# Two-layer decoder trunk on one core: the first mixer's tile slots counted by use, pole scalars in pairs, phase doublings for both layers at once, more gelu copies on ScalarE

## The chip, the core and the metric

The kernel runs on one core of a Trainium2 chip. The time is the device's own, from start to end of one execution, in microseconds (us). Five engines work side by side, each through its own instructions in the order in which they are written, and wait for one another through semaphores: TensorE (PE) multiplies matrices and transposes, VectorE (DVE) and ScalarE (ACT) do elementwise work, GpSimd (POOL) does little here, and SyncE (SP) issues the DMAs. PE's clock is granted by the chip, at full speed (shown as 1.00) or at half of it.

## The reference, cut to what matters

The trunk has two layers of three sub-layers each: a SwiGLU feed-forward block, a mixer, and another feed-forward block, each between two RMS norms and scaled, shifted and gated by rows made from a conditioning vector. There are 256 positions of width 1024, in float32.

```python
for l in range(DEPTH):                       # 2
    x = post_add(x, swiglu(pre(x, 0), ...), 0, FFN_RES)
    y = token_mixer(pre(x, 1), ...)
    x = post_add(x, y, 1, 1.0)
    x = post_add(x, swiglu(pre(x, 2), ...), 2, FFN_RES)

def token_mixer(h, ...):
    u, q, k, v, f, g_a, g_b = split(h @ w_in)
    y_ssm = s5_ssm(u, ...)                   # complex diagonal recurrence over the positions
    z_val, z_gate = split(gelu(y_ssm) @ glu_w)
    y_a = z_val * sigmoid(z_gate)
    y_b = forgetting_attention(q, k, v, f + forget_b) @ attn_w_out
    return (sigmoid(g_a) * y_a + sigmoid(g_b) * y_b) @ w_out
```

`s5_ssm` has 32 groups of 64 complex poles, `lam_bar = exp(lam * dt)`; each state is the last one times `lam_bar` plus an input, and the output is read from the states. The attention has 8 heads of width 64 (4 pairs), with a forget term added to the logits, and a causal mask.

## The kernel before

**Weights.** All weights come as 512 tiles of 128x1024 in one fixed order, `raw0`, `raw1`, ..., each by one DMA. 368 hold weights, 144 ("mod") go into the conditioning rows. To keep float32 precision a weight tile is split: ACT rounds it (`Stream.hi`, line 359, `hi<-raw`), DVE takes the rest (`Stream.lo`, line 372, `lo<-raw,hi`), and PE forms each product in three matmuls, hi·xh, lo·xh and hi·xl. A mod tile costs one DVE instruction (`raw<-raw,crow`, summed into `mc`). SBUF has 42 slots for such tiles (`SLOTS`), shared by the stream and all other big tiles. How far the stream may run ahead is set by `room` (line 351):

```python
return SLOTS - self.kept - (TABLES[self.kb.stage] if self.kb.stage is not None else 0)
```

`kept` is what the stage reserves for itself (`KEPT`), `TABLES` what the building of the recurrence's tables takes in its two stages. At the u projection, before the tables are loaded, `mix_body` (line 946) reserves `KEPT["mix1"] - LATER`.

**The order.** A planner in the kernel (`Plan`, line 164) steps through the program with costs of its own, and writes every engine's instructions in the order in which its clocks would take them. The chip then runs each engine's list strictly in that order, so an instruction that waits holds all behind it. Nearly all instructions are recorded with one line, that of the planner's call, so the names of the tiles tell them apart.

**The mixer.** After the projections v, f, q, k and u come, for each of the four head pairs: scores on PE (`sc<-kt,qt`), the logits' six DVE operations (`lg<-nbd..`), two reduces (`st<-lg`), the exponentials on ACT, a reciprocal on DVE, the normalising on ACT, PE transposes (`sc<-kc,lg`), a copy on ACT (`lg<-sc`), the values on PE (`sc<-lg,v`), and their split into `ath` on ACT and `atl` on DVE. In between PE runs the gate projections ga1, gb0 and gb1 as filler (48 matmuls each; their tiles are 138 to 143, 144 to 149 and 151 to 156). The recurrence takes tables: `bt` turns the spread inputs `U` into `vr` and `vi` (32 matmuls in 16 + 16), `w` is a table of phases that `scan` (line 1257) applies with 12 products of 128x1024 before and after two scans on DVE (first operation `zr<-w,vr`, last one `zr<-zr,t`), `d` adds the part of a chunk's own inputs (`ys<-U,d`), and `c` reads the outputs (`ys<-zr,c`, two groups of 32 matmuls, after the scan). `gelu` (line 1283) takes each half of ys through ACT and copies it to a new layout in 16 small copies of 32x128 (`yg<-g`), then splits it into `ygh` (ACT) and `ygl` (DVE). `yb` is the attention's output projection (tiles 158, 159, 161, 163), `z` the gelu's (tiles 164 to 173), `mt` transposes the merged result, and `ym` is the mixer's output projection. The gating row `gT` is transposed on PE when the mod tiles up to 167 are summed in `mc`.

**Where the tables come from.** `s5_scalars` (line 1384) computes poles, powers and factors for both layers with DVE operations of 128x32, in the first feed-forward block. `s5_tables` (line 1712) builds a layer's tables: layer 0's from the end of that block into mixer 0, layer 1's in the third feed-forward block. Its last step is `s5_w` (line 1540), the phases `wc` and `ws` by six doublings; for five of them the next factor is computed by 11 operations of 128x16 (tile `pw`). The tables are written to HBM and loaded back (`load_tables`, line 1152, and `w<-sw`).

Of the kernel before, what the change touches and what calls it, by code (L numbers as in the profile page):

```python
# [9 lines left out]
F32 = mybir.dt.float32  # L10
F32R = mybir.dt.float32r
I32 = mybir.dt.int32
AF = mybir.ActivationFunctionType
# [25 lines left out]
TABLES = (11, 8)  # L39
# [7 lines left out]
LATER = 4  # L47
# [366 lines left out]
class Kern:  # L414
# [868 lines left out]
    def gelu(self, h, ys, out):  # L1283
# [100 lines left out]
    def s5_scalars(self):  # L1384
# [17 lines left out]
        x1, x2, x3, x4, ur, ui, lre2 = (new() for _ in range(7))  # L1402
# [17 lines left out]
        cth, sth = new(), new()  # L1420
        q, mm_, z = new(), new(), new()
# [41 lines left out]
        def cmul(ore, oim, a, b, t1=t1, t2=t2, t3=t3, t4=t4):  # L1463
            tt(t1, a[0], b[0], M)
            tt(t2, a[1], b[1], M)
            tt(t3, a[0], b[1], M)
            tt(t4, a[1], b[0], M)
            tt(ore, t1, t2, S)
            tt(oim, t3, t4, A)

        LP, NP_, LI = self.spw[:, 0], self.spw[:, 1], self.spw[:, 2]

        def neg(o, a):
            ts(o, a, -1.0, M)

        def powers(i):
            return LP[:, i, :], LI[:, i, :]

        def part3():
            tt(LP[:, 0, :], e, cth, M)  # L1480
            tt(LI[:, 0, :], e, sth, M)
            cmul(*powers(1), powers(0), powers(0))
            cmul(*powers(2), powers(1), powers(0))
            cmul(*powers(3), powers(1), powers(1))
            for i in range(4):
                neg(NP_[:, i, :], LP[:, i, :])
                neg(self.spw[:, 3, i, :], LI[:, i, :])
# [16 lines left out]
        def part5():  # L1504
# [14 lines left out]
            neg(self.sq[:, 2, :], self.sq[:, 1, :])  # L1519
# [20 lines left out]
    def s5_w(self, l):  # L1540
# [5 lines left out]
        p = self.r4("pw")[:, 0:256].rearrange("p (n j) -> p n j", j=16)  # L1546
# [3 lines left out]
        pr, pi = self.sw4[:, 0, 16 * l:16 * l + 16], self.sw4[:, 1, 16 * l:16 * l + 16]  # L1550
        done = v.take()
        for i in range(6):
            n = 1 << i
# [11 lines left out]
            large = v.take()  # L1565
            if i < 5:
                a, b, x, y = (p[:, 4 * (i % 2) + d, :] for d in range(4))
                tt(x, pr, pr, M)
                tt(y, pi, pi, M)
                tt(b, pr, pi, M)  # L1570
                tt(a, x, y, S)
                tt(b, b, b, A)
                tt(x, a, a, M)
                tt(y, b, b, M)
                tt(x, x, y, A)
                v.tensor_scalar(x, x, -0.5, 1.5, op0=M, op1=A)
                tt(a, a, x, M)
                tt(b, b, x, M)
                pr, pi = a, b
            small = v.take()  # L1580
            v.mix(large, small)
            done += v.take()
        v.ops = done
# [80 lines left out]
    def s5_c(self, l):  # L1664
        v3 = lambda c: self.bc[:, 512 + 256 * c:768 + 256 * c].rearrange("p (j n) -> p j n", j=16)
        self.cp = [self.r4(n).rearrange("p (j s n) -> p j s n", j=16, s=4) for n in ("cpr", "cpi")]
        yield from self.powers(self.cp, 0, 4, (v3(0), v3(1)), [self.spw[:, n, :, 16 * l:16 * l + 16] for n in (0, 3, 3, 1)],
# [44 lines left out]
    def s5_tables(self, l):  # L1712
# [25 lines left out]
        if self.s == 1:  # L1738
            self.load_tables()
# [221 lines left out]
```

## Time and profile before

| | us |
|---|---|
| three runs | 1184.0, 1187.42 (median), 1192.24 |
| the profiled execution | 1182.35 |
| span of its records | 1180.6 |
| PE busy | 1140.6 (97%) |
| DVE busy | 912.7 (77%) |
| ACT busy | 608.6 (52%) |
| mean granted clock of PE | 0.992 |

The shares are means over stages that differ: the feed-forward blocks keep PE busy all the time, the mixers don't. A timeline row gives start, duration and instruction, and in brackets how long its engine was idle just before and what ended that. Neighbouring instructions of one engine overlap a little, so the step from one start to the next is shorter than a duration. Times in the rows count from the start of the span.

### The profile page before, as it was taken

How to read it: one execution, taken by the hardware profiler on the slowest of the kernel's cores; microseconds unless marked ns; L12 is line 12 of the kernel's file. 1: busy time of each engine (PE TensorE's matmuls, PEld its weight loads, DVE VectorE, ACT ScalarE, POOL GpSimd, SP SyncE). 2: the span in 40 equal slices, each digit the busy share in tenths (PEclk: the TensorE clock that was granted, in tenths of full speed). 3: DMA queues.
4: the chain of work that ended last, by engine and by line, in shares of the span. 5: the costliest groups of instructions: out<-in, count | busy, mean ns of one | idle time of the engine just before them, and what ended most of it. 6: DMA issues, size and time to landing. Idle time of an engine off the chain costs nothing.

```text
span 1180.6 us, 19407 instructions
## 1 busy us (share of the span) xinstructions
PE 1140.6 (97%) x7488; PEld 1015.5 (86%) x7488; DVE 912.7 (77%) x1529; ACT 608.6 (52%) x943; POOL 36.2 (3%) x62
## 2 busy tenths in 40 slices
PE   8999999998998999999999999999999999999997
PEld 5999998796786779999979989987987887999995
DVE  6988987897998889999678878878448798855532
ACT  5653452685556564444364475356355756543421
POOL 1000000000000010000010000001000001000000
PEclk9999999998999999999999999999999999999999
DMA  9999887577887669999769398966645566765300
GB/s 361 408 367 407 301 286 267 187 257 236 339 306 249 224 235 390 360 376 381 246 214 355 127 330 284 373 248 237 227 127 179 180 212 216 284 224 204 126 19 36
DMA packets 99186, 306.50 MB, mean 260 GB/s; under 512 B 16373, under 2 KB 26133, under 8 KB 99094
## 3 DMA queue, kind: packets, MB, share of 16 engines
q1 hardware_dynamic: 99094, 305.27, 71.6%
q8 instruction: 58, 0.95, 0.3%
q14 instruction: 34, 0.28, 0.1%
HBM read 291.51 MB, written 13.71 MB: 259 GB/s over the span
## 4 chain that ended last, share of the span: by engine, by line
PE 86%; DVE 7%; ACT 3%; DMA 2%; issue 2%; POOL 1%; SPq 0%; DVEq 0%; POOLq 0%; ACTq 0%
PE f L128 35%; PE y L128 20%; PE n L128 5%; PE ym L128 3%; PE ga L128 3%; PE gb L128 3%; PE z L128 3%; PE k L128 2%; PE q L128 2%; PE v L128 2%; PE ys L128 2%; PE u L128 2%; ACT xh L128 1%; DVE raw L128 1%; PE yb L128 1%
## 5 line engine op out<-in xcount | busy, mean ns | idle before, releaser
L128 DVE TENSOR_TENSOR lo<-raw,hi 128x1024 fp32r<-128x1024 f32 x368 | 437.1, 1218 | 27.2 <-ACT hi L128 21.3
L128 ACT ACTIVATE hi<-raw 128x1024 fp32r<-128x1024 f32 x367 | 370.7, 1055 | 68.3 <-PE f L128 38.7
L128 PE MATMUL f<-xl,hi 128*128 128x256 f32 x1216 | 341.4, 281 | 2.7 <-DVE xl L128 2.7
L128 PE MATMUL f<-xh,hi 128*128 128x256 f32 x1216 | 342.0, 281 | 1.9 <-ACT xh L128 1.9
L128 PE MATMUL f<-xh,lo 128*128 128x256 f32 x1216 | 341.0, 280 | 0.0
L128 PEld LDWEIGHTS f<-xh,lo 128*128 128x128 f32 x1216 | 232.4, 191 | 0.0
L128 PEld LDWEIGHTS f<-xl,hi 128*128 128x128 f32 x1216 | 228.4, 188 | 4.6 <-DVE xl L128 3.6
L128 PEld LDWEIGHTS f<-xh,hi 128*128 128x128 f32 x1216 | 228.5, 188 | 3.8 <-ACT xh L128 2.5
L128 PE MATMUL y<-hi,ht 128*128 128x512 f32 x704 | 196.2, 391 | 0.8 <-DVE yg L128 0.8
L128 DVE SCALAR_TENSOR_TENSOR raw<-raw,crow 128x1024 f32<-128x1024 f32 x144 | 173.3, 1218 | 6.0 <-DMA raw<-ws 5.9
L128 PEld LDWEIGHTS y<-hi,ht 128*128 128x128 f32 x704 | 129.3, 188 | 26.2 <-DVE yg L128 1.1
L128 ACT ACTIVATE sg<-f 128x512 f32<-128x512 f32 x38 | 22.7, 597 | 222.7 <-PE f L128 215.4
L128 PE MATMUL y<-lo,ht 128*128 128x512 f32 x352 | 109.3, 390 | 0.8 <-ACT yg L128 0.8
L128 DVE TENSOR_TENSOR sg<-sg,f 128x512 f32<-128x512 f32 x38 | 26.1, 687 | 90.0 <-ACT sg L128 89.9
L128 PEld LDWEIGHTS y<-lo,ht 128*128 128x128 f32 x352 | 66.1, 188 | 15.1 <-ACT yg L128 1.2
L128 PE MATMUL n<-hi,xl 128*128 128x512 f32 x96 | 37.9, 395 | 1.7 <-DVE xl L128 1.7
L128 ACT ACTIVATE lg<-lg,st 128x128 f32<-128x128 f32 (+1 forms) x64 | 26.1, 444 | 25.3 <-DVE st L128 25.3
L128 PE MATMUL n<-hi,xh 128*128 128x512 f32 x96 | 38.4, 400 | 0.0
L128 PE MATMUL n<-lo,xh 128*128 128x512 f32 x96 | 37.7, 392 | 0.0
L128 DVE TENSOR_TENSOR yg<-y,row 128x1024 f32<-128x1024 f32 (+1 forms) x9 | 9.9, 1103 | 32.8 <-ACT xn L128 23.6
L128 DVE TENSOR_TENSOR ht<-sg,ht 128x512 fp32r<-128x512 f32 x38 | 26.1, 687 | 9.8 <-ACT ht L128 9.5
L128 ACT ACTIVATE xh<-xt,mc 128x128 fp32r<-128x128 f32 x80 | 21.7, 383 | 22.1 <-PE xt L128 22.1
(276 smaller groups left out, 1646.7 us busy)
## 6 DMA issues: line engine op xcount, KB each, us to landing
raw<-ws SPq DMA_DIRECT2D x512, 512.0 KB, 5.8
row<-sg SPq DMA_DIRECT2D x11, 512.0 KB, 8.0
sbt<-bT SPq DMA_DIRECT2D x8, 512.0 KB, 3.0
sc<-cd SPq DMA_DIRECT2D x16, 256.0 KB, 8.0
bt<-sbt SPq DMA_DIRECT2D x8, 512.0 KB, 4.5
c<-sc SPq DMA_DIRECT2D x8, 512.0 KB, 10.2
d<-sd SPq DMA_DIRECT2D x4, 512.0 KB, 4.6
w<-sw SPq DMA_DIRECT2D x4, 512.0 KB, 5.8
```

Of the source, the lines that this page charges most:

```text
L128: r = f(*a, **k)
```

## The change

It has three parts.

1. **Slots.** `TABLES` goes from (11, 8) to (9, 0) and `LATER` from 4 to 15. While the layer 0 phases are built, at the u projection, the stream's room is 42 − 8 − 9 = 25 where it was 42 − 19 − 11 = 12 (by the code's own numbers). Before the tables are loaded in a mixer, a loop waits until the slots in use fit.
2. **Scalars.** Real and imaginary parts stand side by side, so that one operation of 128x64 does both (`product`, `square`). Negations and the copies to `srv` go to ACT. All six phase factors are computed for both layers at once in `part4`, 7 rounds of 8 operations, and `s5_w` loses its 110 small operations (55 per layer).
3. **Gelu copies.** 12 of 16 per half run on ACT, 4 on DVE, where it was 8 and 8.

In all DVE has 117 instructions fewer (1386 to 1269, expanded), ACT 22 more (889 to 911), PE, POOL and SP as many as before.

```diff
-TABLES = (11, 8)
+TABLES = (9, 0)
...
+OVER = 0
+LATER = 15
...
-                if t % 2:
+                if t:
                     yield "act", g
                     nc.scalar.activation(o, i, AF.Copy)
...
-        def cmul(ore, oim, a, b, t1=t1, t2=t2, t3=t3, t4=t4):
...
+        def product(out, a, b):
+
+            tt(tp, a, b, M)
+            tt(t3, a[:, 0], b[:, 1], M)
+            tt(t4, a[:, 1], b[:, 0], M)
+            tt(out[:, 0], t1, t2, S)
+            tt(out[:, 1], t3, t4, A)
+
+        def square(out, a, xp=None):
+            x = tp if xp is None else xp
+            tt(x, a, a, M)
+            tt(out[:, 1], a[:, 0], a[:, 1], M)
+            tt(out[:, 0], x[:, 0], x[:, 1], S)
+            tt(out[:, 1], out[:, 1], out[:, 1], A)
...
         def part4():
-            unit = (cth, sth)
-            for out in ((ur, ui), (self.sw4[:, 0, :], self.sw4[:, 1, :])):
-                cmul(lre2, th, unit, unit, x1, x2, x3, x4)
-                tt(x1, lre2, lre2, M)
-                tt(x2, th, th, M)
+            unit = up
+            for i in range(7):
+                out = wp if i == 0 else self.sw4[:, i - 1]
+                square(zp, unit, xp)
+                tt(xp, zp, zp, M)
                 tt(x1, x1, x2, A)
                 ts(x1, x1, -0.5, M, 1.5, A)
-                tt(out[0], lre2, x1, M)
-                tt(out[1], th, x1, M)
+                tt(out, zp, x1[:, None, :].to_broadcast([P, 2, W]), M)
                 unit = out
...
-            for n, src in enumerate((LP, LI, self.spw[:, 3])):
-                for i in range(3):
-                    v.tensor_copy(self.srv[:, n, i, :], src[:, 2 - i, :])
+            for i in range(3):
+                act(self.srv[:, :, i, :], self.spw[:, 1:4, 2 - i, :], AF.Copy)
...
-            if i < 5:
-                a, b, x, y = (p[:, 4 * (i % 2) + d, :] for d in range(4))
...
         if self.s == 1:
+            self.st.kept = KEPT["mix1"]
+            while self.st.used() > SLOTS - self.st.kept + OVER:
+                yield "dve", self.plan.clk["pe"] + 0.5
             self.load_tables()
```

Because the planner writes the order, the first part moves instructions on all engines in mixer 0. On DVE, where the scan starts, before had these rows (`lo` with its `raw` tile's number; `st` are the softmax's sums):

```order
L128 TENSOR_REDUCE st_508_3594<-lg_507_3593 128x2 x2
L128 TENSOR_SCALAR st_508_3594<-st_508_3594 128x4
L128 TENSOR_TENSOR lo_509_3604<-raw146_435_3011,hi_495_3540 128x1024
L128 TENSOR_TENSOR lo_510_3610<-raw148_454_3186,hi_500_3550 128x1024
L128 RECIPROCAL st_508_3594<-st_508_3594 128x4
L128 TENSOR_TENSOR lo_511_3613<-raw149_455_3188,hi_503_3580 128x1024
L128 TENSOR_TENSOR zr_492_3536<-w_489_3529,vr_487_3447 128x1024
L128 TENSOR_TENSOR t_494_3538<-w_490_3531,vi_488_3448 128x1024
```

In the changed order the low parts of tiles 149 to 163, the mod rows 152 to 167 and the softmax of head pair 2 come first. From the middle of that stretch:

```order
L129 TENSOR_TENSOR lo_522_3602<-raw158_472_3249,hi_520_3594 128x1024
L129 SCALAR_TENSOR_TENSOR raw157_470_3242,mc_82<-raw157_470_3242,crow_73 128x1024
L129 SCALAR_TENSOR_TENSOR raw160_490_3400,mc_82<-raw160_490_3400,crow_73 128x1024
L129 SCALAR_TENSOR_TENSOR raw162_501_3505,mc_82<-raw162_501_3505,crow_73 128x1024
L129 TENSOR_TENSOR lo_534_3674<-raw159_489_3398,hi_532_3670 128x1024
L129 TENSOR_TENSOR atl_493_3442<-sc_496_3461,ath_492_3441 128x256
L129 TENSOR_TENSOR lo_538_3701<-raw161_495_3452,hi_536_3697 128x1024
L129 SCALAR_TENSOR_TENSOR raw165_511_3565,mc_82<-raw165_511_3565,crow_73 128x1024
```

After it come the six logits' operations of pair 2, and then the end of the stretch:

```order
L129 TENSOR_REDUCE st_541_3710<-lg_540_3709 128x2 x2
L129 TENSOR_SCALAR st_541_3710<-st_541_3710 128x4
L129 SCALAR_TENSOR_TENSOR raw167_516_3581,mc_82<-raw167_516_3581,crow_73 128x1024
L129 TENSOR_TENSOR mc_82<-mc_82,kc_74 128x8
L129 SCALAR_TENSOR_TENSOR mc_82<-mc_82,kc_74 128x8
L129 RECIPROCAL st_541_3710<-st_541_3710 128x4
L129 TENSOR_TENSOR lo_546_3752<-raw163_505_3532,hi_544_3748 128x1024
L129 TENSOR_TENSOR zr_529_3647<-w_526_3640,vr_518_3591 128x1024
```

The scan's first product moved behind the low parts of 151 to 163 and the sums of head pair 2; the mod row 167 and its `mc`, which stood behind the gelu, moved ahead of it.

On ACT, these rows of the changed order feed that stretch (`lg<-sc` is the copy of a head pair's transposes, here pair 1's; `ath` the split of its values):

```order
L129 ACTIVATE hi_515_3579<-raw156_469_3238 128x1024
L129 ACTIVATE hi_520_3594<-raw158_472_3249 128x1024
L129 ACTIVATE lg_497_3468<-sc_496_3461 128x2x384
L129 ACTIVATE hi_532_3670<-raw159_489_3398 128x1024
L129 ACTIVATE ath_492_3441<-sc_496_3461 128x256
L129 ACTIVATE hi_536_3697<-raw161_495_3452 128x1024
```

In before, hi of 159 came after the copy of pair 3's transposes, and its lo after the scan.

On PE, between the last gate matmuls and the first matmuls that need the scan (`ys<-zr,c`), before had:

```order
L128 MATMUL gb1_530_3736<-hi_524_3693,xl_72 128x512
L128 MATMUL ys_544_3838<-U_468_3281,d_461_3231 128x64 x8
L128 MATMUL ys_544_3838<-U_468_3281,d_462_3232 128x64 x8
L128 MATMUL yb_547_3861<-hi_532_3757,ath_481_3414 128x512 x2
L128 MATMUL yb_547_3861<-lo_540_3817,ath_481_3414 128x512 x2
L128 MATMUL yb_547_3861<-hi_532_3757,atl_482_3415 128x512 x2
L128 MATMUL ys_544_3838<-zr_492_3536,c_512_3624 128x63
```

and the changed order has:

```order
L129 MATMUL gb1_513_3569<-hi_515_3579,xl_72 128x512
L129 MATMUL ys_551_3767<-U_474_3291,d_483_3367 128x64 x8
L129 MATMUL ys_551_3767<-U_474_3291,d_484_3368 128x64 x8
L129 MATMUL sc_535_3695<-kc_74,lg_540_3709 128x128 x6
L129 MATMUL sc_552_3791<-kt_442_3061,qt_411_2861 128x128 x2
L129 MATMUL sc_552_3791<-kt_442_3061,qt_411_2861 128x256 x2
L129 MATMUL sc_535_3695<-lg_540_3709,v_343_2423 64x128 x6
L129 MATMUL sc_552_3791<-kc_74,lg_554_3798 128x128 x6
L129 MATMUL sc_552_3791<-lg_554_3798,v_343_2423 64x128 x6
L129 MATMUL yb_557_3848<-hi_520_3594,ath_492_3441 128x512 x2
L129 MATMUL yb_557_3848<-lo_522_3602,ath_492_3441 128x512 x2
L129 MATMUL yb_557_3848<-hi_520_3594,atl_493_3442 128x512 x2
```

Nine more yb rows follow, and then `ys<-zr,c`. The last two head pairs and twelve yb rows, where it was three, now stand ahead of the scan's first reader. Two further moves on PE are not shown: the 32 matmuls of vr and vi, which stood ahead of the last quarter of ga1, now stand behind all of ga1 and gb0 and the first quarter of gb1; and gT stands in the middle of z where it stood behind it.

## Rows read from the trace of the kernel before

**Rows 1.** The page's part 1: busy us (share of the span), instructions.
```profile
PE 1140.6 (97%) x7488; PEld 1015.5 (86%) x7488; DVE 912.7 (77%) x1529; ACT 608.6 (52%) x943; POOL 36.2 (3%) x62
```

**Rows 2.** Windows: from:to us, length, busy us (instructions) by engine, clock, DMA, GB/s.
```profile
46.00:206.00 160.00, 160.00 (x1122) 149.46 (x1121) 138.13 (x276) 74.88 (x95) 1.77 (x5) 1.00 0.90 332
236.00:394.00 158.00, 141.87 (x952) 121.58 (x951) 141.54 (x300) 99.45 (x185) 1.16 (x2) 0.97 0.78 276
620.00:797.00 177.00, 176.38 (x1271) 162.52 (x1271) 146.53 (x260) 94.21 (x138) 2.36 (x4) 1.00 0.78 286
```

**Rows 3.** PE's waits: who waited for whom, total us, times, longest.
```profile
PE z L128 <- ACT ygh L128: 4.8, 1, 4.8
...
PE gT L128 <- DVE mc L128: 2.8, 1, 2.8
...
PE ga L128 <- DVE lo L128: 2.3, 1, 2.3
...
PE ga L128 <- ACT hi L128: 1.4, 1, 1.4
...
PE z L128 <- DVE ygl L128: 0.5, 1, 0.5
```

**Rows 4.** PE's timeline, mixer 0: start us, us, instruction, [idle before].
```profile
276.89 0.50 PE L128 MATMUL ga<-hi,xh 128*128 128x512 f32 x1
...
295.49 0.43 PE L128 MATMUL vr<-U,bt 128*128 128x64 f32 x2
...
302.68 0.82 PE L128 MATMUL sc<-kc,lg 128*128 128x128 f32 x6
...
344.04 0.43 PE L128 MATMUL ys<-zr,c 128*128 128x63 f32 x2 [0.64 <-DVE zr L128]
...
371.28 1.22 PE L128 MATMUL z<-hi,ygh 128*128 128x512 f32 x2 [4.79 <-ACT ygh L128]
...
393.03 0.70 PE L128 MATMUL ym<-hi,xh 128*128 128x512 f32 x2
```

**Rows 5.** The chain of waits, mixer 0: start us, us, what.
```profile
286.88 5.06 PE ga L128 x11
...
296.25 1.55 DVE lg L128 x6
297.80 0.93 DVE st L128 x2
...
298.96 1.87 ACT lg L128 x8
...
310.93 5.80 DMA w<-sw
...
329.14 2.77 PE gb L128 x12
```

**Rows 6.** DVE's timeline in the first scan.
```profile
315.06 1.21 DVE L128 TENSOR_TENSOR zr<-w,vr 128x1024 f32<-128x1024 f32 x1
...
327.73 1.22 DVE L128 TENSOR_TENSOR zi<-zi,t 128x1024 f32<-128x1024 f32 x1
328.87 2.28 DVE L128 TENSOR_TENSOR_SCAN zr<-r,zr 128x1024 f32<-128x1024 f32 x1
...
342.77 1.22 DVE L128 TENSOR_TENSOR zr<-zr,t 128x1024 f32<-128x1024 f32 x1
```

**Rows 7.** ACT's timeline, beside it.
```profile
315.47 1.99 ACT L128 ACTIVATE hi<-raw 128x1024 fp32r<-128x1024 f32 x2
...
326.93 1.49 ACT L128 ACTIVATE lg<-lg,st 128x128 f32<-128x128 f32 x4
```

**Rows 8.** Tile pw, all operations: count, duration ns min/median/max, first and last start.
```profile
L128 DVE TENSOR_TENSOR pw<-pw x94: 143/166/178, 274.4 to 767.2; 128x16 f32<-128x16 f32 x94
```

**Rows 9.** Tile yg, the two kinds of gelu copy, same columns.
```profile
L128 ACT ACTIVATE yg<-g x32: 424/430/441, 348.5 to 940.5; 32x128 f32<-32x128 f32 x32
L128 DVE COPY yg<-g x32: 266/274/279, 351.9 to 941.3; 32x128 f32<-32x128 f32 x32
```

More of the change, by code (lines that the diff above doesn't have):

```diff
@@ L46 @@
 NEAR = 1
-LATER = 4
+OVER = 0
+LATER = 15
 SCAN, GELU, MERGE, TR = 0.5, 0.95, 0.5, 1.5
@@ L1401, in s5_scalars @@
         t1, t2, t3, t4 = new(), new(), new(), new()
-        x1, x2, x3, x4, ur, ui, lre2 = (new() for _ in range(7))
+        x1, x2, x3, x4, ur, ui, lre2, th2 = (new() for _ in range(8))
+        pair = lambda n: T[:, n:n + 2, :]
+        tp, xp, wp, zp = pair(4), pair(8), pair(12), pair(14)
         def exp(out, x):
@@ L1420, in s5_scalars @@
         cth, sth = new(), new()
+        up = pair(16)
         q, mm_, z = new(), new(), new()
@@ L1461, in part2 @@
             tt(sth, sth, z, A)
-        def cmul(ore, oim, a, b, t1=t1, t2=t2, t3=t3, t4=t4):
[L1464 to L1474, printed above, removed]
+        def product(out, a, b):
[10 more added lines that the diff above has]
+            tt(out[:, 1], out[:, 1], out[:, 1], A)
+        act = lambda *a, **k: v.ops.append((self.nc.scalar.activation, a, k))
+        NP_, LP, LI, NI = (self.spw[:, i] for i in range(4))
         def powers(i):
-            return LP[:, i, :], LI[:, i, :]
+            return self.spw[:, 1:3, i, :]
         def part3():
@@ L1481, in part3 @@
             tt(LI[:, 0, :], e, sth, M)
[L1482 to L1487, printed above, removed]
+            square(powers(1), powers(0))
+            product(powers(2), powers(1), powers(0))
+            square(powers(3), powers(1))
+            act(NP_, LP, AF.Copy, scale=-1.0)
+            act(NI, LI, AF.Copy, scale=-1.0)
             r4 = self.sr4.rearrange("p l j -> p (l j)")
@@ L1518, in part5 @@
             tt(self.sq[:, 1, :], t3, q, M)
-            neg(self.sq[:, 2, :], self.sq[:, 1, :])
+            act(self.sq[:, 2, :], self.sq[:, 1, :], AF.Copy, scale=-1.0)
         def part6():
-            for n, src in enumerate((LP, LI, self.spw[:, 3])):
-                for i in range(3):
-                    v.tensor_copy(self.srv[:, n, i, :], src[:, 2 - i, :])
+            for i in range(3):
+                act(self.srv[:, :, i, :], self.spw[:, 1:4, 2 - i, :], AF.Copy)
         def part(*fs):
@@ L1549, in s5_w @@
         tt = lambda o, a, b, op: v.tensor_tensor(o, a, b, op=op)
-        pr, pi = self.sw4[:, 0, 16 * l:16 * l + 16], self.sw4[:, 1, 16 * l:16 * l + 16]
-        done = v.take()
         for i in range(6):
+            pr, pi = (self.sw4[:, i, k, 16 * l:16 * l + 16] for k in range(2))
             n = 1 << i
@@ L1564, in s5_w @@
             tt(s1, s1, t2, A)
-            large = v.take()
-            if i < 5:
-                a, b, x, y = (p[:, 4 * (i % 2) + d, :] for d in range(4))
[L1568 to L1583, printed above, removed]
         yield from v.run()
@@ L1666, in s5_c @@
         self.cp = [self.r4(n).rearrange("p (j s n) -> p j s n", j=16, s=4) for n in ("cpr", "cpi")]
-        yield from self.powers(self.cp, 0, 4, (v3(0), v3(1)), [self.spw[:, n, :, 16 * l:16 * l + 16] for n in (0, 3, 3, 1)],
+        yield from self.powers(self.cp, 0, 4, (v3(0), v3(1)), [self.spw[:, n, :, 16 * l:16 * l + 16] for n in (1, 3, 3, 0)],
                     self.r4("ct"))
@@ L1761, in run @@
             self.sq = cst.tile([P, 3, 32], F32, name="sq")
-            self.sw4 = cst.tile([P, 2, 32], F32, name="sw4")
+            self.sw4 = cst.tile([P, 6, 2, 32], F32, name="sw4")
             self.sr4 = cst.tile([P, 2, 16], F32, name="sr4")
```

1 line of the change is left out of this document (removed).

## The prediction

> **What bounds the kernel now.** The page's first part comes first: TensorE (PE) is busy for 1140.6 of 1180.6 us, VectorE (DVE) for 912.7, ScalarE (ACT) for 608.6 [rows 1]. So nothing that shortens DVE or ACT can pay unless PE waits for them, and all that can be won is 40 us of PE idle plus what a low clock costs. Then the windows say where PE waits. In the first feed-forward stage (46 to 206) it is busy for 160.00 of 160 us, in a later one (620 to 797) for 176.38 of 177; from the first mixer's last third of projections to the end of its gates (236 to 394) for 141.87 of 158, at a granted clock of 0.97, with DVE busy for 141.54 [rows 2]. Here DVE is as full as PE, and the two wait for each other. The list of PE's waits names the places: z for the rounded gelu output ygh 4.8 us, the row transpose gT for mc 2.8, ga for lo 2.3 and for hi 1.4 [rows 3]. The chain adds one: after ga's wait eleven matmuls took 5.06 us, where twelve of the same shape take 2.77 [rows 5]; that is the 1.2 GHz level of the clock, some 2.5 us lost.
>
> All of this lies in mixer 0, and the change edits mixer 0. Outside it I read the edits as hidden.
>
> **Edits outside the mixer: 0.** The pair packing, the negations on ACT and the doublings for both layers stand in the first feed-forward stage. DVE loses 23 small operations there and gains 32; at 0.17 us, the nearest recorded size [rows 8], the nine more are +1.5 us, with bounds of −4 (the 32 as good as free) and +5 (none saved). DVE has 22 us of slack in that stage and PE has none [rows 2], so nothing moves; if the cover were gone it would be those 1.5 us. ACT gets 6 copies on 75 us of work in 160. Layer 1's table phases lose 55 operations of 128x16, 94 recorded for both layers at 166 ns [rows 8], in the stage where PE is busy for 176.38 of 177 us: hidden too.
>
> **Edits in mixer 0, walked by hand.** I took the changed order of PE, DVE and ACT, gave each instruction the start-to-start time of its like in the trace of before, and let each start when its engine and its inputs are free. PE: a 512-wide matmul 0.229, so 12 are 2.75 [rows 5]; the 32 vr/vi are 7.2 (295.49 to 302.68), a transpose set or scores about 0.9 [rows 4]. DVE: a 1024-wide operation 1.14, a scan 2.2 [rows 6]; the six lg operations 1.55 and their two reduces 1.0 [rows 5]. ACT: the exponentials of one head pair 1.87 [rows 5], hi or a copy of its size 1.0, normalising 1.4 [rows 7].
>
> *The front.* ga1 starts at 276.89 [rows 4]. All its low parts now stand ahead of the table phases on DVE, so its 48 matmuls run through to about 288.0: the 1.4 and 2.3 us waits and the slow clock, 6.2 us, are gone. Waits for the softmax of pair 0 (2.1) and the score sets bring PE to 293.2; 24 of gb0 to 298.7; a wait for lo148, behind the phases, 1.3; the rest of gb0 and 12 of gb1 to 307.9; vr/vi to 315.1. In before vr/vi were done at 302.68 [rows 4], since they stood ahead of those 36 gate matmuls.
>
> *The scan start.* This is the term that decides. DVE runs the low parts up to lo158, then lo159. Its input hi159 stands on ACT behind the copy lg<-sc of pair 1, which waits for PE's transposes of pair 1, which stand behind vr/vi. Transposes 315.9, copy 316.7, hi159 317.7, lo159 318.9; atl after values(1) 320.3; lo161 and a mod row 323.2. Scores(2) end on PE at 323.2, lg and reduces at 326.0, exponentials 327.9, the gb1 copy 328.9, normalising 330.3, hi163 331.3, lo163 332.5. Only then does DVE reach zr<-w,vr, the scan's first product; in before it starts at 315.06 [rows 6]. So the scan starts 17.4 us later. It then has less between its operations: 12 products and 2 scans are 18.1, one lg set 2.6, two atl 0.7, one low part 1.1, small waits 1.0, together 23.5, against 28.9 in before (315.06 to 342.77 and the last product's 1.22), which has five low parts in it. It ends at 356.0, 12 later than 344.0.
>
> *After the scan.* PE waits meanwhile (about 3 us for the gb1 copy, 3 for scores(3), 6.7 for pair 3's normalising, 3 for atl), all under the scan. The scan's first consumers in before started at 344.04 [rows 4], now at 356.1: +12.1. Of the 24 double yb matmuls that before put between and behind the ys groups, 9 doubles (18 single) more are done earlier: −4.1. z then starts at 368.9 instead of 360.9, eight late. In before it ran into ygh at 366.5 and waited 4.8, with the clock low for 3.4 us after it (1.22 us for the pair of matmuls that takes 0.70 at ym; I count 1.7 lost), and later 2.8 at gT [rows 3, 4]. Now gT's rows are finished in the scan's shadow (mod row 167 ends near 328): −2.8. For the ygh wait, the moved copies count.
>
> *The copies.* ACT takes 12 of 16 copies per half at 430 ns, where DVE needs 274 [rows 9], so 4 more on ACT are +1.7 us on the engine that ygh stands on, and DVE is rid of 4 × 0.274. From the first ys group's end (359.8) on: gelu 0.6, 12 copies 5.2, the second gelu, ygh(0) 0.6 to 366.9, then 12 copies 5.2, five hi 5.0, ygh(1) 0.6: 377.8. z's first 24 matmuls end at 374.3, so it waits 3.5, some 0.4 more for ygl, and perhaps again a slow stretch (0 to 1.7). This replaces before's 4.8 + 1.7.
>
> The overview of the engines speaks against this edit: the Trainium skill, "Trainium Architecture — The Big Picture", section "The five engines, in one table", lists simple arithmetic as what ScalarE is not for, VectorE being up to about 3 times faster per element. The trace shows 430 against 274 ns for these copies, 1.6 times [rows 9]. At three times (an estimate from that page: 0.82 us a copy) ygh(1) would come some 9 us later and the sum be +12; the recorded 430 ns are ACT's own in this very place, so the trace decides.
>
> **Sum of mixer 0**: +12.1 (scan) −4.1 (yb done earlier) −6.5 (old ygh wait and clock) −2.8 (gT) +3.9 (new ygh and ygl wait) + 0 to 1.7 (clock) = +2.6 to +4.3. The 6.2 us won at the front are in the scan's start already and buy nothing: PE waits for the scan afterwards. In mixer 1 the ygl wait of 0.5 [rows 3] may go: −0.5. I take **+3 us**: 1182.35 of the profiled execution becomes 1185.4, and as the median of the runs shown, 1187.42, stands 0.43% above that execution, 1190.4, rounded **1190**.
>
> Bounds of what no row shows. The 17.4 us rest on one order of waits; a hi earlier by a slot would give 3 to 4 us of them back, while the reloaded phase table w, which took 5.80 us to land [rows 5], now queues behind nine weight tiles and could be the last instead. I put it at 318 to 320, 12 us ahead of need.
>
> **Rivals.** About 1%, or 12 us, is what a measurement of this kernel tells from no change.
> - *The weights-first order pays (faster, but within 1%).* If the scan starts near 320, since PE and ACT run through their filler faster than I stack them, it ends where it did (12.1 becomes 0), and the other terms stay: −4.1 −6.5 −2.8 +3.9 = −9.5, 1178. For it: DVE loses 55 small operations just here, near 6 us. Against: lo159 waits for vr/vi whatever DVE saves. More than 12 us faster would need most of the 16 us that PE idles in 236 to 394, and the clock's loss.
> - *The scan gets later still (slower).* Every us after 332.5 moves the end one for one. If w lands behind the nine weight tiles only at 343, as the DMA queue is held by tile slots that DVE frees and DVE by w, the sum is +3 + 10.5 = +13.5, 1201. It decides from a landing at 332.5 on, and passes 1% from about 341. Against: the earlier landing that I put above.
> - *The deeper stream does not form.* If the new count leaves ga1's waits where they were, PE is 6 us late into vr/vi as well and the scan by as much: +9, 1196. The written order speaks against it.
> - *The copies are dearer on ACT.* If twelve in a row took twice 430 ns, ygh(1) would come 24 × 0.43 = 10 us later: +13, 1200. Against: the 32 recorded ones spread only from 424 to 441 ns [rows 9].
>
> **Numbers.** Forecast (+3, between −3 and +8) 0.65; front pays 0.16; deeper stream fails 0.05; dearer copies 0.02; scan later still 0.12. Faster by over 1%: a third of the second case and the tail of the first, 0.08. Slower by over 1%: scan later still, dearer copies where they pass 12 us, a little of the third, 0.13. Same: 0.79. The range goes from 1177 (the second case) to 1200 (just short of the scan's case).
>
> **What would show it.** ga's waits near 283 gone and no half clock there; vr/vi ending near 315; zr<-w,vr starting within 3 us of 332.5 with lo163 as its predecessor; PE's waits of some 6 us for normalised lg or zi; z waiting for ygh 3 to 4 us; no gT wait; ym starting near 396 (before 393.03 [rows 4]). A scan start before 325 makes me wrong to the fast side; a DVE wait for w, or ym after 403, to the slow side.

## The result, and the profile after

The changed kernel takes 1191.68 us (median of 20 runs, 1189.84 to 1195.29), the kernel before, measured beside it, 1183.5 us (20 runs). The ratio on record is 1.0051, 95% interval 1.0034 to 1.0069: some 6 us slower, or half a per cent. The two medians by themselves are 8.2 us apart, a quotient of 1.0069, which is the upper end of that interval. The profiled execution of the changed kernel took 1193.02 us, with a span of 1191.2.

The page's first part, as in [rows 1]:

```profile
PE 1149.9 (97%) x7488; PEld 1024.2 (86%) x7488; DVE 901.8 (76%) x1412; ACT 616.9 (52%) x965; POOL 36.6 (3%) x62
```

DVE works 10.9 us less, as the packing meant it to. PE has the same 7488 instructions and is busy 9.3 us longer: it ran more of them at half clock. The windows say where (columns as in [rows 2]); the first, third and last answer to [rows 2], the others cut single places out:

```profile
46.00:206.00 160.00, 159.84 (x1120) 149.23 (x1119) 141.13 (x282) 76.89 (x102) 2.13 (x5) 1.00 0.89 333
206.00:236.00 30.00, 27.45 (x125) 21.65 (x126) 23.65 (x41) 18.89 (x37) 2.35 (x4) 0.94 0.53 181
236.00:394.00 158.00, 139.51 (x910) 119.82 (x908) 126.30 (x226) 96.08 (x186) 1.17 (x2) 0.90 0.72 260
293.00:299.00 6.00, 3.90 (x24) 2.99 (x26) 6.00 (x25) 4.97 (x9) 0.00 (x0) 0.59 0.71 223
335.00:347.00 12.00, 10.81 (x58) 9.59 (x58) 8.79 (x13) 4.59 (x9) 0.00 (x0) 0.57 0.92 358
620.00:797.00 177.00, 175.85 (x1268) 161.60 (x1267) 143.76 (x212) 92.45 (x140) 1.57 (x2) 1.00 0.78 287
```

The feed-forward stages are as full as before. Mixer 0 is not: from 236 to 394 DVE is busy for 126.30 us where it was 141.54, PE's instructions are 910 where they were 952, and the clock is 0.90 where it was 0.97. PE's waits, by the rows that have a part in mixer 0:

```profile
PE sc L129 <- ACT lg L129: 14.3, 8, 4.5
PE z L129 <- ACT ygh L129: 3.9, 1, 3.9
...
PE ys L129 <- ACT gb L129: 2.8, 1, 2.8
...
PE ys L129 <- DVE zr L129: 0.5, 1, 0.5
```

The waits of ga and gT [rows 3] are gone; the largest sum is now for the softmax's normalised logits (`sc` for `lg`): 11.3 of the 14.3 us, in six waits, lie between 236 and 394, and the rest is mixer 1's. PE's timeline, with the starts that answer to [rows 4]:

```profile
293.77 0.33 PE L129 MATMUL sc<-kc,lg 128*128 128x128 f32 x1 [4.27 <-ACT lg L129]
294.46 1.33 PE L129 MATMUL sc<-kc,lg 128*128 128x128 f32 x5 [0.37 <-ACT lg L129]
296.75 1.55 PE L129 MATMUL sc<-lg,v 128*64 128x128 f32 x12 [0.96 <-ACT lg L129]
298.23 1.66 PE L129 MATMUL sc<-kt,qt 64*128 64x128 f32 x8
...
314.15 0.33 PE L129 MATMUL vr<-U,bt 128*128 128x64 f32 x2
...
362.98 0.43 PE L129 MATMUL ys<-zr,c 128*128 128x63 f32 x2 [0.46 <-DVE zr L129]
...
385.19 0.73 PE L129 MATMUL z<-hi,ygh 128*128 128x512 f32 x2 [3.86 <-ACT ygh L129]
...
404.53 0.62 PE L129 MATMUL ym<-hi,xh 128*128 128x512 f32 x2
```

And DVE's, where the wait begins and where the scan stands (compare [rows 6]):

```profile
287.77 0.35 DVE L129 SCALAR_TENSOR_TENSOR lg<-nbd,cq,sc 128x128 f32<-128x128 f32 x1 [2.09 <-DMA sc<-cd]
...
323.89 1.23 DVE L129 TENSOR_TENSOR lo<-raw,hi 128x1024 fp32r<-128x1024 f32 x1 [4.07 <-ACT hi L129]
...
337.49 1.23 DVE L129 TENSOR_TENSOR lo<-raw,hi 128x1024 fp32r<-128x1024 f32 x1 [3.05 <-ACT hi L129]
338.63 1.22 DVE L129 TENSOR_TENSOR zr<-w,vr 128x1024 f32<-128x1024 f32 x1
...
361.71 1.22 DVE L129 TENSOR_TENSOR zr<-zr,t 128x1024 f32<-128x1024 f32 x1
```

ga starts at 278.23 in the changed kernel and at 276.89 before [rows 4]: 1.34 us were lost earlier, by a stretch at half clock at 206 to 236. The same window of before ran at full clock:

```profile
206.00:236.00 30.00, 27.29 (x138) 21.77 (x138) 24.95 (x40) 20.73 (x40) 2.35 (x4) 1.00 0.56 190
```

PE waits in it for the same 0.46 and 1.46 us at the first v matmuls in both kernels, and only in the changed one did half clock follow. Counted from ga's start, the mixer goes like this (the last column is the change against before):

| us after ga's start | before | changed | |
|---|---|---|---|
| scan starts (`zr<-w,vr`) | 38.2 | 60.4 | +22.2 |
| scan ends (`zr<-zr,t`) | 67.1 | 84.7 | +17.6 |
| z starts | 84.0 | 97.5 | +13.5 |
| ym starts | 116.1 | 126.3 | +10.2 |

So 10.2 us were lost between ga and ym, where the whole span grew by 10.6; of the 1.34 lost earlier, most came back behind ym. The two spans are one execution each; the 6 us of the ratio, from 20 runs of each, are the better size.

### The profile page after: what moved, and what is told of

Its sections match the earlier page's. It is cut to its first block, busy times and chain, and to the rows that moved or that the text cites. A ratio compares the mean times of both kernels' runs of the same rounds, so it can differ in the third digit from the quotient of the medians.

```text
span 1191.2 us, 19323 instructions
## 1 busy us (share of the span) xinstructions
PE 1149.9 (97%) x7488; PEld 1024.2 (86%) x7488; DVE 901.8 (76%) x1412; ACT 616.9 (52%) x965; POOL 36.6 (3%) x62
## 4 chain that ended last, share of the span: by engine, by line
PE 84%; DVE 6%; ACT 5%; DMA 2%; issue 1%; POOL 1%; SPq 0%; DVEq 0%; POOLq 0%; ACTq 0%
PE f L129 34%; PE y L129 19%; PE gb L129 4%; PE n L129 4%; PE ym L129 3%; PE z L129 3%; PE ga L129 3%; PE v L129 2%; PE q L129 2%; PE ys L129 2%; PE sc L129 1%; ACT xh L129 1%; PE k L129 1%; DVE raw L129 1%; DVE lo L129 1%
## 5 line engine op out<-in xcount | busy, mean ns | idle before, releaser
L129 DVE TENSOR_TENSOR ht<-sg,ht 128x512 fp32r<-128x512 f32 x38 | 26.1, 688 | 10.9 <-ACT ht L129 10.7
L129 ACT ACTIVATE xh<-xt,mc 128x128 fp32r<-128x128 f32 x80 | 21.7, 383 | 21.6 <-PE xt L129 21.6
## 6 DMA issues: line engine op xcount, KB each, us to landing
w<-sw SPq DMA_DIRECT2D x4, 512.0 KB, 10.7
```

What stands on the lines that cost most here:

```text
L129: r = f(*a, **k)
```

## The experiments

Three theories stood at the start. By the *scan theory* the loss is the scan that starts later because the gate projections and low parts were put ahead of it. By the *front theory* it is the wait at the softmax of pair 0, which the forecast had too short. By the *copies theory* it is ACT's twelve gelu copies. Two more, the *work theory* and the *chain theory*, came with the last four runs. The kernel before had a median of 1185.82, 1185.85 and 1185.08 us beside the three groups of runs. Times after ga's start in this table are read from the timelines as in the one above. The last column lists every wait of over 0.2 us that ACT or DVE shows in its timeline, from 276 us to z, whose releaser is a DMA that *writes* a table or the mask bias to HBM (`snb<-cumt`, `sc<-cd`, `sd<-kt`, `sw<-wc`).

| run | ratio, 95% interval | scan starts | scan ends | ym | waits for a write |
|---|---|---|---|---|---|
| before | 1 | 38.2 | 67.1 | 116.1 | none |
| changed | 1.0051, 1.0034 to 1.0069 | 60.4 | 84.7 | 126.3 | snb 3.11, sc 2.09 |
| slots alone | 1.0037, 1.0012 to 1.0063 | 57.8 | 82.6 | 122.0 | snb 4.78, sd 2.54 |
| packing and doublings alone | 1.0014, 0.9994 to 1.0034 | 47.9 | 76.6 | 118.7 | none |
| packing, doublings, copies | 1.0012, 0.9992 to 1.0032 | 49.1 | 77.8 | 119.6 | none |
| all but the copies (8 and 8) | 1.0073, 1.0050 to 1.0097 | 60.8 | 84.9 | 129.3 | snb 3.44, sc 2.15 |
| mask bias first | 1.0086, 1.0055 to 1.0116 | 63.2 | 87.2 | 129.4 | sc 3.77 |
| `LATER` 4 | 1.0076, 1.0052 to 1.0100 | 51.1 | 87.3 | 131.8 | sw 10.32 |
| bt loaded first | 1.0153, 1.0109 to 1.0196 | 51.7 | 90.2 | 138.4 | snb 3.39, sc 2.11, sd 3.62 |
| bt first and `LATER` 4 | 1.0089, 1.0062 to 1.0115 | 52.4 | 87.1 | 130.4 | sw 9.71 |
| vr and vi early | 1.0168, 1.0137 to 1.0199 | 57.7 | 98.2 | 142.9 | snb 3.41, sc 2.16 |
| mod rows behind the scan | 1.0174, 1.0119 to 1.0230 | 68.0 | 97.9 | 139.2 | snb 2.93, sc 1.92, sw 10.21 |
| mod rows and ao parts behind | 1.0183, 1.0136 to 1.0229 | 67.5 | 97.6 | 140.2 | snb 2.99, sc 1.91, sw 10.23 |
| the same with `LATER` 4 | 0.9990, 0.9965 to 1.0015 | 44.3 | 74.3 | 118.7 | none |

Two columns carry it. The ratio goes with the scan's end and not with its start: three kernels start the scan some 8 to 9 us earlier than the changed one and are slower. Up to an end at 77.8 no loss can be told; from 82.6 on it is there, and largest where the scan ends last. And the three versions without a wait for a write are the three whose interval holds 1; the ten with one are all slower. Two of these three count the slots as before, so only the last row speaks for the waits within the new count. The size of the loss doesn't follow the sum of the waits: vr and vi early has 5.6 us of them and a ratio of 1.0168, `LATER` 4 has 10.3 us and 1.0076.

### The parts one by one

**Slots alone.** The kernel before, with `TABLES`, `LATER` and the loop of part 1.

```diff
-TABLES = (11, 8)
+TABLES = (9, 0)
...
-LATER = 4
+LATER = 15
...
+            self.st.kept = KEPT["mix1"]
+            while self.st.used() > SLOTS - self.st.kept + OVER:
+                yield "dve", self.plan.clk["pe"] + 0.5
```

> The first part of the change alone on the kernel before: TABLES (9, 0), LATER 15 and the waiting loop; scalars, the 110 small operations and the copies as before. The order of PE is that of the changed kernel but for three yb rows. If the slots carry the loss, the ratio to before is 1.004 to 1.012, the more since the small operations still stand between the low parts; if they are harmless and another part costs, 1.002 or less.

Measured 1.0037, with an interval above 1: a little under the range for "the slots carry the loss", and clear of no loss. **Packing and doublings alone** is the changed kernel without part 1 (table reserves of 12 and 8 in place of the 11 and 8 of before, `LATER` back at 4, no loop) and with the copies at 8 and 8:

```diff
-TABLES = (9, 0)
+TABLES = (12, 8)
-LATER = 15
+LATER = 4
...
-            while self.st.used() > SLOTS - self.st.kept + OVER:
-                yield "dve", self.plan.clk["pe"] + 0.5
...
-                if t:
+                if t % 2:
```

> The second part of the change alone: packed scalars, doublings for both layers, gelu copies 8 and 8, LATER 4, no waiting loop, the table stage's reserve 12 and 8 (before: 11 and 8), so the stream stays about as shallow as before and vr/vi stand behind half of ga1. Scan theory: the scan starts within 3 us of before's 315.06 and the time is before's or a little less: ratio 0.994 to 1.001. If the packing or the moved scalar work itself costs time: ratio over 1.003.

Measured 1.0014, an interval that holds 1. The scan, though, starts 9.7 us later after ga than in the kernel before, not within 3 as expected, and ends 9.5 later, and the time is the same: z starts 9.5 us later, and ym 2.6. So a late scan alone doesn't cost the 6 us. Half clock alone doesn't either. This is the run's window from ga's start to the scan's end, at a clock of 0.84, the same as in the changed kernel (its row is the first of the pair of windows further down):

```profile
278.70:355.30 76.60, 64.71 (x344) 53.62 (x342) 60.83 (x104) 40.34 (x86) 1.94 (x2) 0.84 0.81 295
```

**With the copies at 12 and 4** added to that:

> Packing, doublings and the 12/4 split of the gelu copies, with the slots counted as before. Packing and doublings alone measured 1.0014. If the slots carry the loss: 0.997 to 1.002. If the copies on ScalarE cost time where yb is not done earlier: 1.004 or more.

Measured 1.0012. **All but the copies**, the changed kernel with the last edit of the diff above (`if t % 2`) alone:

> The changed kernel with its gelu copies back at 8 on ScalarE and 8 on VectorE per half; slots, packing and doublings stay. If the scan's late start sets the end of mixer 0 (scan theory), only z's wait for ygh shrinks, from 3.9 us to 1 to 2, and the scan still starts near 338: 2 to 3 us under the changed kernel, a ratio to before of 1.003 to 1.005. If the moved copies are what costs (copies theory), the time falls back to before: ratio 1.000 or less.

Measured 1.0073, above what either theory expected. The copies theory falls: taken back, they make nothing faster, and z then waits 5.1 us for the two halves of the gelu output (1.07 + 3.14 + 0.91) in place of 3.86. The new count of the slots carries a loss of its own, and the packing and doublings neither cost nor win what this measurement can tell. They take 8.6 us of DVE's work out of the stretch to the scan's end; this is what the windows of the changed kernel and then of the slots alone show (DVE is the third busy time):

```profile
278.23:362.93 84.70, 70.20 (x362) 56.73 (x360) 68.20 (x134) 38.67 (x85) 1.17 (x2) 0.84 0.79 287
```

```profile
279.85:362.45 82.60, 67.24 (x368) 53.48 (x366) 76.76 (x193) 39.07 (x85) 1.89 (x2) 0.90 0.79 295
```

The idle time, the stretch less DVE's busy time, went from 5.84 to 16.50 us: all 8.6 us became idle, and 2.1 us more (one execution each; the two ratios, 1.0037 and 1.0051, have intervals that overlap). In this order DVE's work is not what the scan waits for.

### The front

The chain of the changed kernel says what the softmax of pair 0 waited for:

```profile
270.04 7.87 DMA snb<-cumt
...
279.83 7.81 DMA sc<-cd
287.77 1.64 DVE lg L129 x6
...
299.88 14.43 PE gb L129 x60
```

`sc<-cd` writes a table to HBM. The logits take over a tile slot, and by the releaser in the trace it is the slot of that table: they can't be written until the write has landed. In the kernel's code `cumt`, `cd`, `kt`, `wc` and `ws`, which such writes read, and `hi`, `lo`, `lg` and `gb`, which take slots over, are all tiles of one pool (`r4`, line 422 in before). SyncE's timeline of before and of the changed kernel:

```profile
257.09 4.12 SPq L128 DMA_DIRECT2D raw<-ws  x7
...
268.28 0.32 SPq L128 DMA_DIRECT2D snb<-cumt  x1
272.41 0.33 SPq L128 DMA_DIRECT2D nbp<-snb  x1
...
273.31 0.94 SPq L128 DMA_DIRECT2D sc<-cd  x2
...
275.82 12.75 SPq L128 DMA_DIRECT2D sd<-kt  x16
```

```profile
255.49 1.46 SPq L129 DMA_DIRECT2D raw<-ws  x2
...
258.37 7.40 SPq L129 DMA_DIRECT2D raw<-ws  x9
...
270.04 1.01 SPq L129 DMA_DIRECT2D snb<-cumt  x1
277.97 0.33 SPq L129 DMA_DIRECT2D nbp<-snb  x1
...
278.83 0.90 SPq L129 DMA_DIRECT2D raw<-ws  x2
279.83 1.41 SPq L129 DMA_DIRECT2D sc<-cd  x2
...
288.02 12.46 SPq L129 DMA_DIRECT2D sd<-kt  x16
...
324.27 1.83 SPq L129 DMA_DIRECT2D w<-sw  x2
```

From the issue of `snb` to that of `nbp`, which reads it back, are 4.1 us in before and 7.9 in the changed kernel; from the table's write to the next writes (`sd`) 2.5 and 8.2. Thirteen weight tiles are issued ahead of the table's write in these rows, where it was seven: the room won for the stream was filled with loads, and the small round trips stand behind them. In the last row the phase table `w` is read back; a later point rests on it.

**Mask bias first.** The larger room is opened only behind the DMAs of the mask bias.

```diff
-        self.st.kept = KEPT["mix1"] - (0 if self.bt else LATER)
+        self.st.kept = KEPT["mix1"] - (0 if self.bt else 4)
...
+        if late and not self.bt:
+            self.st.kept = KEPT["mix1"] - LATER
+            self.st.pump()
```

> The changed kernel in which the stream gets its larger room in layer 0 only once the three mask-bias DMAs are issued, so two weight tiles fewer stand ahead of them; the place of vr/vi and the scan's place in VectorE's order are as in the changed kernel. Scan theory: tr(0)'s wait of 4.6 us shrinks to 1 to 3, and the scan's start and the end move by the same 2 to 4 us: ratio to before 1.001 to 1.004. Front theory: the whole loss goes: ratio 1.000 or less. Neither, if the wait of lg(0) is for the slot that a table's write to memory holds: no gain, 1.005 to 1.008.

The mask bias was ready at 281.53, but the first logits began at 287.01 after 3.77 us for `sc<-cd`: the slot, not the bias, held them. The transposes of pair 0 waited 6.7 us, the scan began 2.8 us later after ga than in the changed kernel, and ym 3.1: here the front went through one for one. The third outcome, a wait for the slot of a table's write and no gain, is what came, with 1.0086 a little over its range.

**`LATER` 4**, the stream's room at the u projection as in the kernel before as far as `LATER` goes:

```diff
-LATER = 15
+LATER = 4
```

> The changed kernel with LATER back at 4: at the u projection the stream's room is 14 instead of 25, so the mask bias and the table writes stand ahead of tile 149 on the DMA queue, and vr/vi behind a quarter of gb0. Both theories expect a gain here, of different size. Front theory: tr(0)'s wait shrinks to 1 to 2 us and the slow clock after it goes; with it the loss: ratio to before 0.998 to 1.002. Scan theory: the same, and the scan ends as much earlier as it starts, near 350: ratio 0.990 to 0.997. Above 1.003 both fail.

The front was as the front theory wants it: no wait of the transposes for pair 0, scores of pair 1 done at 294.5. The scan started 9.3 us earlier after ga. Yet it ended 2.6 us later, and the ratio was 1.0076. PE's waits of this run show what came in:

```profile
PE z L129 <- ACT ygh L129: 8.0, 1, 8.0
PE sc L129 <- DVE atl L129: 7.4, 1, 7.4
```

From PE the wait leads back through `atl` and a low part on DVE to this row of ACT:

```profile
317.61 1.06 ACT L129 ACTIVATE hi<-raw 128x1024 fp32r<-128x1024 f32 x1 [10.32 <-DMA sw<-wc]
```

ACT stood 10.3 us until the phase table `wc` was written: by that releaser the rounded weight tile takes over the table's slot. The ratio is above 1.003, so by their own measure both fail: the front theory as the only cause, and the scan theory in its form "the start decides". The wait for a slot had moved from the table `cd` to the table `wc`.

**bt first, and the same with `LATER` 4.** The four loads of bt are issued ahead of the sixteen `sd` writes, so that vr and vi don't wait for them.

```diff
+            early = self.load_bt()
+        self.s5_place(l, kt)
...
+            self.load_tables(early)
```

> The changed kernel in which the four bt loads are issued ahead of the 16 sd writes instead of behind them (the waiting loop stands ahead of both), so that vr/vi need not wait for them; by the planner's order vr/vi then stand behind half of gb0, and four low parts fewer ahead of the scan. The front (tr(0) behind the mask bias and the table write) stays. Scan theory: tr(0) still waits 4 to 5 us, vr/vi run without a wait from about 306 to 313, the scan ends near 352 instead of 362.9 and the time falls by 8 to 11 us: ratio to before 0.995 to 0.999. Front theory: the time stays, 1.005 to 1.008.

> e5 and e6 together: the changed kernel with LATER 4 and the bt loads ahead of the sd writes. Scan theory: the earliest scan start of these, near 318, and a ratio to before of 0.985 to 0.994. Front theory: the same as with LATER 4 alone, within 2 us.

Measured 1.0153 and 1.0089. The first is outside both theories' ranges; the second has the median of `LATER` 4 alone within 0.1 us, the number that the front theory expected, though its front doesn't wait. In the first, vr and vi ran without a wait from 305.95 to 313.21 and the scan began 8.7 us earlier than in the changed kernel, but DVE then stood idle for 10.9 us inside it, ACT had waited 3.6 us for an `sd` write, and z waited 11.6 us for ygh. The second has the wait for `wc` again, 9.71 us. **vr and vi early**: layer 0 issues one filler step and then vr, where it filled until bt was there.

```diff
-        self.fill(lambda: self.begun() and self.there(*bt[0], *bt[1])())
+        if l == 0:
+            self.fill_one()
+        else:
+            self.fill(lambda: self.begun() and self.there(*bt[0], *bt[1])())
```

> The changed kernel with the 32 vr/vi matmuls of layer 0 behind the first quarter of gb0 instead of behind gb0 and a quarter of gb1; everything else as the planner then writes it. Scan theory: vr/vi end near 310 instead of 321, the scan starts near 325 instead of 338.6, and with it all after the scan comes some 10 us earlier: ratio to before 0.995 to 1.001. Front theory (the mask bias that lands 6 us later, and the slow clock after it, are the cost): tr(0) still waits 4 to 5 us and the time stays: ratio 1.005 to 1.008.

Measured 1.0168, outside both ranges. vr and vi waited for bt (0.80 + 3.31 us), then ran at half clock until 319.54; inside the scan the logits of pair 3 waited 10.95 us for PE. An earlier start moved the waits into the scan.

### What stands ahead of the scan's end

Two theories were left. *Work*: the mod rows that now stand ahead of the scan, seven by the changed kernel's timeline (9.1 us with their accumulator reads), cost what they take. *Chain*: the scan waits for lo159 and lo163, and rows ahead of it only fill that wait. **Mod rows behind the scan:**

```diff
-        return ("dve", self.plan.ready([self.mods[0][1]])) if self.mods else (None, 0.0)
+        return ("dve", self.plan.ready([self.mods[0][1]])) if self.mods and not self.kb.hold else (None, 0.0)
...
+        self.hold = l == 0
...
+            if len(ops) <= 0:
+                self.hold = False
```

> The changed kernel with mixer 0's sixteen modulation rows (152 to 167, the part that stood ahead of the first scan, about 8 us of DVE) held back until the scan has been issued; PE's order nearly the same (15 double yb matmuls ahead of ysc). Work theory (the scan's end is set by what DVE does ahead of it, and the rows that the new order puts there are 8 to 9 us of it): scan end 6 to 9 us earlier than in the changed kernel, counted from the first gate matmul (84.7 there), ratio 0.995 to 0.999 of the kernel before. Chain theory (the scan waits for lo159 and lo163, behind hi and the softmax; DVE's work ahead only fills its waits): DVE idles instead, scan end within 3 us of 84.7, ratio 1.002 to 1.007.

**The low parts of the output projection too:**

```diff
-        if not self.raw or self.used() >= self.room() and len(self.fresh) + len(self.split) > 1:
+        if not self.raw or self.kb.hold and self.raw[0][0][0] == "ao" or self.used() >= self.room() and len(self.fresh) + len(self.split) > 1:
```

> As the run with the modulation rows behind the scan, and the high and low parts of the four output-projection tiles (158, 159, 161, 163) held back as well, so that the scan's first product waits for no low part. yb then has only 9 rows ahead of ysc and its rest, 6.5 us of PE, goes behind. Work theory: the scan starts and ends some 4 to 8 us earlier than with the modulation rows alone, and yb's later work gives part of it back: ratio 0.994 to 1.000. Chain theory: the scan starts 10 us or more earlier (lo159 and lo163 were what held it), end 10 us earlier, 6.5 given back: 0.995 to 1.001. If the scan's END stays within 3 us of 84.7 after the first gate matmul although its start moves, what holds the end is inside the scan (pair 3's lg, its waits), and the ratio is 1.004 or more.

Measured 1.0174 and 1.0183; both theories missed by far. In the windows from ga's start to the scan's end DVE is busy for 60.0 and 58.0 us, where the changed kernel has 68.2, and with vr and vi early these are the slowest of all. The piece of the first one's chain and the row of ACT that explain it:

```profile
299.34 5.62 DMA bt<-sbt
305.03 12.07 DMA sw<-wc
317.18 1.03 ACT gb L129
```

```profile
317.18 1.02 ACT L129 ACTIVATE gb<-gb 128x1024 f32<-128x1024 f32 x1 [10.21 <-DMA sw<-wc]
```

Here it is the gate's tile gb that took the slot of `wc`, and its write took 12.07 us, with four weight tiles issued in the 4 us ahead of it. ACT stood, PE stood 5.7 us ahead of vi, then ran 62 matmuls at half clock from 318.26 to 331.75. As tests of work against chain the two are spoilt; instead they add a wait of 10.2 us to the suspected cost, and by the ratios the time grows by some 15 us against the changed kernel. **The last run** cuts the stream's room back as well, `LATER` 4 with both holds:

> As the last run, and the share of tile slots given to later tiles cut from 15 to 4, which in an earlier run let lg of pair 0 start without waiting for its slot but put a wait of 7.4 us for atl in its place, behind modulation rows. With those rows held that wait has no cause. If work and waits of DVE ahead of the scan's end are what costs: scan end 60 to 70 us after the first gate matmul (67.1 in the kernel before), ratio 0.990 to 0.997. If the time is set elsewhere (by yb, the gelu copies or the output projection behind the scan): ratio 0.999 or more with a wait of z for ygh of 8 us or more.

Measured 0.9990, interval 0.9965 to 1.0015: the time of the kernel before, by the two ratios 0.6% under the changed kernel and 0.9% under `LATER` 4 without the holds. It lies between the two outcomes expected: the scan ended at 74.3 and not at 60 to 70, and z waited 2.8 us in all for ygh and not 8. ACT and DVE wait for no write from 276 us to z. Outside that stretch two such waits are left, and the changed kernel has both: 1.45 us at 264 for `sbt<-bT` (1.17 there), and 3.33 at 766 for layer 1's `sw<-wc` (3.59 there), in a stage where PE is full. Its chain:

```profile
270.39 5.01 DMA snb<-cumt
...
310.45 10.09 DMA sw<-ws
320.60 6.30 DMA w<-sw
```

The phase table's write is as slow as in the other runs, 10.09 us, but what it delays is only the table's own read-back, for which the scan's first products wait 2.2 and 2.9 us. This version doesn't beat the kernel before, and no other run did.

What this shows: the loss comes with the new count of the slots, which alone costs time (1.0037, interval 1.0012 to 1.0063), and not with the other two parts. Every version of the new count that waits in mixer 0 for a slot that a write to HBM still holds is slower than before, and the one that doesn't wait is not. What is not shown is that these waits are the cause: that last version also holds back the mod rows and the parts of four tiles and ends the scan 10 us earlier, each edit reorders the rest, and the loss doesn't grow in step with the waits. How much of the 6 us is the waits and how much the order behind them stays open. That the larger reserve of the kernel before works as a cushion, by which a slot has rested before it is taken again, is my reading of this; no run changes the slots' rotation alone.

## Why the prediction was right, and where it was off

The sign, the size within its range and the place were right: +3 us, 1190, range 1177 to 1200, all of it in mixer 0; measured 6 us by the ratio and 1191.68. That 1190 came so near is in part luck: it was counted up from 1187.42, the median of three runs, which stands 3.9 us above the median of the twenty, and +3 on 1183.5 would have been 1186.5. In the profiled executions, which the walk describes, +10.7 us stand against +3. Point by point, with times from ga's start, so that the 1.34 us lost earlier don't count:

- **Edits outside the mixer: 0.** Held: 159.84 and 175.85 us of PE in the windows of 160 and 177, with DVE 3 us more in the first and 2.8 less in the second.
- **The front.** "Its 48 matmuls run through" held: ga has no wait and no half clock. "Waits for the softmax of pair 0 (2.1) and the score sets bring PE to 293.2", or 16.3 after ga, is **the step that was off**: the scores of pair 1 end at 299.89, 21.7 after ga. The waits are 4.27 + 0.37 + 0.96 = 5.6 us in place of 2.1, and the window of 293 to 299 shows a clock of 0.59. The two make up the 5.4 us. The walk let each operation start when its engine and its *inputs* are free; it had no line for the slot of its output. The wait for lo148 (1.3) didn't come. (The forecast's own terms give 308.2 for its 307.9 ahead of vr/vi, a slip of 0.3.)
- **The scan start.** Forecast 55.6 after ga (332.5), measured 60.4. It stands where the text put it, behind lo159 (4.07 us for hi) and lo163 (3.05 us for hi), and the delay of 4.8 is the front's, handed on. **In the scan**: 24.3 us against the forecast 23.5, with 7.09 us for the 32 `ys<-U,d` at half clock.
- **After the scan.** From the first `ys<-zr,c` to z are 12.75 us, as forecast (356.1 to 368.9), 4.1 less than before. z waits 3.86 for ygh; forecast were 3.5 and 0.4 more. gT doesn't wait. From z to ym are 28.8 us; forecast 27.1, and the low clock that the text let stand at 0 to 1.7 can take the rest.

The sum with the measured terms: scan end +17.6 (forecast +12.1), yb −4.1, z to ym −3.3 (forecast −5.4 to −3.7), in all +10.2 in the profiled execution. The terms came in the order and for the waits that the forecast named, and the first was mis-sized by 5.5, nearly all of it at the front. By the forecast's own signs this is the slow side: ym starts at 404.53, or 403.2 less the 1.34, where it had named 403, and `zr<-w,vr` lies 4.8 us off its 332.5, where it had allowed 3. The +10.2 don't make the front the one cause either: with `LATER` 4 it came out as forecast, and a wait of the same kind further on took the gain.

Of the rivals, "the weights-first order pays" fell: the scan didn't start near 320, and an earlier start didn't pay by itself in three runs. "The scan gets later still" came in part, by 4.8 us, but not by w, for which DVE didn't wait. This was close. The forecast had w land at 318 to 320, 12 us ahead of need. The write `sw<-wc`, issued at 307.52, took 12.3 us to land, the read-back was issued from 324.27 on, and its second half, issued at 325.6, landed after 10.7 us, near 336.3: 3.5 us ahead of the product that reads it (`t<-w,vi`, at 339.76). With the scan at the forecast 55.6 after ga, this product would have stood at 334.9 and waited some 1.4 us for w (an estimate from these rows). That the rival cost nothing is luck, since the longer front had put the scan back by more. "The deeper stream does not form" fell with ga's missing waits. "The copies are dearer" fell:

```profile
L129 ACT ACTIVATE yg<-g x48: 422/428/442, 367.4 to 952.4; 32x128 f32<-32x128 f32 x48
L129 DVE COPY yg<-g x16: 266/276/281, 367.4 to 950.7; 32x128 f32<-32x128 f32 x16
```

Twelve in a row take 428 ns each on ACT, the 430 of [rows 9], and DVE 276: 1.55 times, against the factor of up to about 3 per element that the Trainium skill, "Trainium Architecture — The Big Picture", section "The five engines, in one table", gives for simple arithmetic. For copies this small the trace doesn't bear that factor out, and the measurement decides.

## What to carry to other kernels

Room for a deeper stream is filled with loads, and the small round trips through memory then stand behind them: here the mask's write to its read-back went from 4.1 to 7.9 us, and a tile slot that such a write reads from is held as long. Look for both before a reserve is cut. When an order is walked by hand, give each operation a third time beside its engine's and its inputs': when the slot of its output comes free, and by which DMA. And work taken off an engine that waits in a chain can become idle time: with 8.6 us less on DVE the scan ended no earlier here.

## What the runs showed that was not expected

The phase tables' writes took 3.34 us in the kernel before (`sw<-ws`), and 10.09 (`sw<-ws`) and 12.07 us (`sw<-wc`) in the chains of the two runs with the new slot count shown above. In before the last weight tile ahead of them is issued 11 us before `sw<-wc`; in those runs eleven and four tiles are issued, the last of them about 1 us ahead of `sw<-wc`. That the tiles make the writes slow is a reading, which no run tests alone. The row of before:

```profile
307.51 3.34 DMA sw<-ws
```

A wait can cost PE twice: after 4.27 us of waiting for pair 0 it was granted 0.59 on average over the next stretch, and after 2.77 us of waiting for gb 0.57, so that the 32 matmuls of `ys<-U,d` took 7.09 us. It doesn't always: the waits at the first v matmuls, the same in both kernels, were followed by half clock in one and by full clock in the other. In the whole stretch from ga's start to the scan's end PE was busy for 70.2 us in the changed kernel and 58.6 in the kernel before, for 362 recorded instructions and 344.
